# A hybrid decoder layer on one core: a fourth wide block product in the up projections, and a final norm split over two banks

## The chip, the cores and the metric

The kernel runs on one NeuronCore of a Trainium2 chip. The metric is the device time of one execution in microseconds (us). Five engines matter: TensorE (PE) multiplies matrices into PSUM banks, VectorE (DVE) and ScalarE (ACT) work on tiles of 128 rows, GpSimd (POOL) and SyncE (SP) issue transfers here. Each engine takes its instructions in the order in which the program gives them, and waits at one whose inputs aren't there yet.

## The reference, cut to what matters

One layer of 1024 columns over 512 positions in float32: a gated feed-forward block, a mixer, a second gated feed-forward block, and a root-mean-square norm. The change touches the up projections of both feed-forward blocks and the very end.

```python
def rmsnorm(x, g):
    x32 = x.astype(jnp.float32)
    y = x32 * lax.rsqrt(jnp.mean(x32 * x32, axis=-1, keepdims=True) + EPS)
    return (y * g.astype(jnp.float32)).astype(x.dtype)

def swiglu(x, w_gate, w_up, w_down):
    return (jax.nn.silu(x @ w_gate) * (x @ w_up)) @ w_down

x = x + 0.5 * swiglu(rmsnorm(x, ffn1_norm[l]), ffn1_wg[l], ffn1_wu[l], ffn1_wd[l])
x = x + hybrid_mixer(rmsnorm(x, mix_norm[l]), w_in[l], ...)
x = x + 0.5 * swiglu(rmsnorm(x, ffn2_norm[l]), ffn2_wg[l], ffn2_wu[l], ffn2_wd[l])
return rmsnorm(x, final_norm)
```

## The kernel before

*Three products for one.* Every float32 matrix is split into a rounded part and the rest: weights into `wh` (ACT copies, rounding) and `wl` (DVE subtracts: `wl = w - wh`), operands likewise into two halves of a tile `cm`: columns `lo` (0 to 255) hold the rounded part, columns `hi` (256 to 511) the rest. A product is `wh x lo + wh x hi + wl x lo`, three matmuls of 256 columns for a weight tile.

*Block products.* The up projection (`ffn_up`, L378) multiplies pairs of weight blocks by a scheme with seven block products instead of eight, numbered p = 1 to 7. A "set" `w` is one pair of blocks of the gate matrix (even `w`, `o.j` = 0) or of the up matrix (odd `w`, `o.j` = 1). The first projection has 16 sets, the second 18 (`count`). The list `stream` (L451 to 456) gives the order of the products of all sets: 1, 2 of set w, 4 of set w-1, 6 of w, 3 of w-1, 5 and 7 of w; each set adds seven. In the loop over `stream`, step i issues on PE the four weight tiles of product i (`products`, L482), then on ACT and DVE what follows from product i-1 (`results`, L510), then the split into `wh` and `wl` for product i+4 (`prepare`, L469; `LEAD` is 4), with the sum of weight blocks that the product after needs (`add_weights`, L459: `s`). In the first few rounds of 14 products one older result is split as well (`halve`, L600, every 14th step while i // 14 is under 6 in the first projection and under 4 in the second). The order is written out by hand, each engine's queue is the order of the program.

*Wide products.* Where `wide(p, w)` (L506) holds, the two matmuls that share `wh` are one of 512 columns over `lo` and `hi`, into both halves of a bank, and the halves are added later by DVE. Before, this is so for products 2, 5 and 3 (`WIDE`, L48), which have banks of the pool `aux`; product 4 goes, with 1, 6 and 7, into the bank `o.beta` of the pool `mm`, a running sum that ACT or DVE reads after each of them.

*What follows a product.* `o.t1` and `o.t2` hold a set's results (tiles `tg` for even sets, `tu` for odd ones). After product 4 an even set's Silu is taken by ACT from the bank, and an odd set's DVE multiplies the bank with the even set's Silu into `h2`. After product 3, ACT takes the Silu of `o.t1` (even) or DVE multiplies `h1` (odd).

*The end.* The second down projection ends with product 4 of its own block scheme, eight steps for row blocks m = 0 and 1; the last three (`TAIL`, L46) are done for m = 0 first and then for m = 1. Then (L1733 on) DVE adds each block's bank to the residual `xr`, the squares are summed (ACT for m = 0, DVE for m = 1), `norm_root` (L1682) takes the root on ACT and the reciprocal on DVE, and `scaled` (L1693) makes the two output halves of a row block, one on ACT and one on DVE, and issues their transfers.

Of the kernel before, what the change touches and what calls it, by code (L numbers as in the profile page):

```python
# [9 lines left out]
F32 = mybir.dt.float32  # L10
F32R = mybir.dt.float32r
AF = mybir.ActivationFunctionType
ALU = mybir.AluOpType

P = 128
S = 512
D = 1024
# [6 lines left out]
QB = 128  # L24
# [18 lines left out]
WARM = 8  # L43
HS = S // 2
LEAD = 4
PLAIN, PAIRS, TAIL = 6, 8, 3  # L46
DIRECT = 4
WIDE, FIRST_WIDE = (2, 5, 3), 2  # L48


ORDER = """
# [126 lines left out]
def hybrid_kernel(ctx, tc, xt, vec, w1u, w1d, wm, wki, wrg, watt, wrnn, wout, w2u, w2d, gf, out):  # L178
    nc = tc.nc
    plan = Plan()  # L180
    V, A = plan.engine("DVE", nc.vector), plan.engine("ACT", nc.scalar)
    G, T = plan.engine("POOL", nc.gpsimd), plan.engine("PE", nc.tensor)
    Q = plan.engine("SP", nc.sync)
# [16 lines left out]
    def nm(s):  # L200
        cnt[0] += 1
        return f"{s}_{cnt[0]}"

    def slot(dt=F32, name="s"):
        return plan.take("slot", big.tile([P, S], dt, tag="slot", name=nm(name)))

    def work(name="t", cols=S):
        return plan.take("tmp", tmp.tile([P, cols], F32, tag="tmp", name=nm(name)))

    def awork(name="a"):  # L210
        return patt.tile([P, S], F32, tag="att", name=nm(name))

    def psum(tag="mm"):
        return psp.tile([P, S], F32, tag=tag, name=nm(tag))
# [100 lines left out]
    lo, hi = slice(0, HS), slice(HS, S)  # L315
# [62 lines left out]
    def ffn_up(y, wu, n0, hs, g, waiting=(), given=(), ahead=None):  # L378
# [10 lines left out]
        ws = []  # L389
# [65 lines left out]
        w = count - 1  # L455
        stream[-3:] = [(5, w), (7, w), (3, w - 1), (4, w), (3, w)]
        units = []
# [52 lines left out]
        def results(i):  # L510
            p, w = stream[i]
            o = ws[w]
            if p == 1:
                o.t1, o.t2 = (work("tg"), work("tg")) if o.j == 0 else (awork("tu"), awork("tu"))
                A.activation(o.t1[:, lo], o.beta[:, lo], AF.Copy)
            elif p == 2:
                V.tensor_sub(o.t1[:, lo], o.p2[:, lo], o.t1[:, lo])
                if wide(2, w):
                    V.tensor_add(o.t1[:, lo], o.p2[:, hi], o.t1[:, lo])
            elif p == 6:  # L520
                A.activation(o.t1[:, hi], o.beta[:, lo], AF.Copy)
            elif p == 7:
                A.activation(o.t2[:, hi], o.beta[:, lo], AF.Copy)
                V.tensor_add(o.t2[:, hi], o.gamma[:, lo], o.t2[:, hi])
                if wide(5, w):
                    V.tensor_add(o.t2[:, hi], o.gamma[:, hi], o.t2[:, hi])
                if o.j:
                    o.h2 = slot(F32, "h")
                    V.tensor_mul(o.h2[:, hi], o.t2[:, hi], ws[w - 1].t2[:, hi])
                else:  # L530
                    A.activation(o.t2[:, hi], o.t2[:, hi], AF.Silu)
            elif p == 4:
                if o.j:
                    V.tensor_mul(o.h2[:, lo], o.beta[:, lo], ws[w - 1].t2[:, lo])
                else:
                    A.activation(o.t2[:, lo], o.beta[:, lo], AF.Silu)
            elif p == 3:
                V.scalar_tensor_tensor(o.t1[:, hi], o.gamma[:, lo], -1.0, o.t1[:, hi], op0=ALU.mult, op1=ALU.subtract)
                if wide(3, w):
                    V.tensor_sub(o.t1[:, hi], o.t1[:, hi], o.gamma[:, hi])  # L540
                if o.j:
                    o.h1 = slot(F32, "h")
                    V.tensor_mul(o.h1, o.t1, ws[w - 1].t1)
                    hs.extend((o.h1, o.h2))
                else:
                    A.activation(o.t1, o.t1, AF.Silu)

        with tc.manual_schedule(engines=ENGINES):
            for _ in range(len(raws), RAWS + len(raws)):
# [3 lines left out]
            for d, (n, j) in enumerate(direct):  # L553
# [5 lines left out]
                steps = [results_direct(d - 1)] if d else []  # L559
# [210 lines left out]
    for k in range(KD):  # L770
        if k:
            Q.dma_start(x[k], xt[k])
        if k % CH == 0:
            c = slice(k * P, (k + CH) * P)
# [14 lines left out]
    for k in range(KD):  # L789
        y.append(norm_tile(k, V_G1, False))  # L790
        if k % CH == 0:
            c = slice(k * P, (k + CH) * P)
# [4 lines left out]
    pu, w = psum(), given(AH[0])  # L797
# [86 lines left out]
    steps, index, last = d1.steps, d1.index, len(d1.steps) - TAIL  # L884
# [70 lines left out]
    with tc.manual_schedule(engines=ENGINES):  # L955
# [3 lines left out]
        for i in range(last):  # L959
            if i == 0:  # L960
                for k in ("pth", "ptl"):
                    t = ptp.tile([P, NQ * S], F32, tag=k, name=nm("sm"))
# [285 lines left out]
    for k in ("pth", "ptl"):  # L1248
        q = ptp.tile([P, NQ * S], F32R, tag=k, name=nm("QI"))
# [341 lines left out]
    steps, index, units, turned, tasks_at = d2.steps, d2.index, d2.units, d2.turned, d2.tasks_at  # L1591
# [15 lines left out]
    def chain(p, m):  # L1607

        key = CHAIN.get(p, p), m
        if key not in banks:  # L1610
            banks[key] = psum("aux" if p == 2 else "mm")
        return banks[key]

    def products(i, ms=range(2)):
        h, l = (t[:, i % 2 * S:(i % 2 + 1) * S] for t in units[i // 2])
        if steps[i][0] == "D":
            _, half, k = steps[i]
            hh, hl = hs[k]
            for m in range(NQ):
                if k == 0:  # L1620
                    banks["D", half, m] = psum("aux")
                c, o = slice(m * QB, (m + 1) * QB), banks["D", half, m]
                T.matmul(o, hh[:, c], h, start=k == 0, stop=False)
                T.matmul(o, hl[:, c], h, start=False, stop=False)
                T.matmul(o, hh[:, c], l, start=False, stop=k == PLAIN - 1)
            return
        p, j = steps[i]
        t, starts = turned[p, j], p in (1, 2, 5)
        opens = dict(skip_group_check=not starts)
        for m in ms:  # L1630
            o, th, tl = chain(p, m), t[:, m * QB:(m + 1) * QB], t[:, HS + m * QB:HS + (m + 1) * QB]
            T.matmul(o, th, h, start=starts and j == 0, stop=False, **opens)
            T.matmul(o, tl, h, start=False, stop=False, **opens)
            T.matmul(o, th, l, start=False, stop=j == PAIRS - 1, **opens)

    def rows(m, half):
        return xr[m // 2][:, m % 2, half * S:(half + 1) * S]

    def results(i):
        st = steps[i]  # L1640
        if st[0] == "D":
            if st[2] == PLAIN - 1:
                for m in range(NQ):
                    r = rows(m, st[1])
                    V.scalar_tensor_tensor(r, banks["D", st[1], m], 0.5, r, op0=ALU.mult, op1=ALU.add)
            return
        p, j = st
        if j == PAIRS - 1:
            for s_, half, sign in ADDS[p]:
                for m in range(2):  # L1650
                    r = rows(2 * s_ + m, half)
                    V.scalar_tensor_tensor(r, chain(p, m), 0.5 * sign, r, op0=ALU.mult, op1=ALU.add)

    gb = []
# [8 lines left out]
    def squares(m, half, ss, E=A):  # L1663
        sq, r = work("sq"), rows(m, half)
        if E is A:
            A.activation(sq, r, AF.Square, accum_out=ss)
        else:
            V.tensor_tensor_reduce(sq, r, r, 1.0, 0.0, ALU.mult, ALU.add, ss)

    norms = {}  # L1670
# [11 lines left out]
    def norm_root(m):  # L1682
        ss = norms[m]
        A.activation(ss[:, 3:4], ss[:, 2:3], AF.Sqrt, scale=1.0 / D, bias=ss[:, 1:2])
        rs = norms[m] = st_("rs", "m8")
        V.reciprocal(rs[:, 0:1], ss[:, 3:4])
# [6 lines left out]
    def scaled(m, E=Q):  # L1693

        rs, o = norms[m][:, 0:1], [slot(F32, "o") for _ in range(2)]
        A.activation(o[0], rows(m, 0), AF.Copy, scale=rs)
        E.dma_start(out[m * QB:(m + 1) * QB, :S], o[0])
        V.scalar_tensor_tensor(o[1], rows(m, 1), rs, gb[1], op0=ALU.mult, op1=ALU.mult)
        Q.dma_start(out[m * QB:(m + 1) * QB, S:], o[1])
# [14 lines left out]
    ffn_up(y2, w2u, 0, hs, V_G2, ahead=tasks_at)  # L1714
    with tc.manual_schedule(engines=ENGINES):
        assert min(d2.tasks) >= 0
        for i in range(len(steps) - TAIL):
            if i < KD // 2:
                turn(2 * i)
                turn(2 * i + 1)  # L1720
            products(i)
            if i:
                results(i - 1)
            if i == 8:
                gains()
            tasks_at(i)
            for f_, args in late.pop(i, ()):
                f_(*args)
        results(len(steps) - TAIL - 1)
        assert not late  # L1730

        for m in range(2):
            for i in range(len(steps) - TAIL, len(steps)):  # L1733
                products(i, (m,))
        for m in range(2):
            r = rows(m, 1)
            if m:
                norm_root(0)
            V.scalar_tensor_tensor(r, chain(4, m), 0.5, r, op0=ALU.mult, op1=ALU.add)
            squares(m, 1, norms[m][:, 2:3], (A, V)[m])  # L1740
        scaled(0, nc.scalar)
        norm_root(1)
        scaled(1, nc.scalar)


def _tiles(w, kt, m=P):
# [55 lines left out]
```

## Time and profile before

| | |
|---|---|
| time, median of 3 runs (lowest to highest) | 1063.77 us (1063.01 to 1063.98) |
| the profiled execution, its own time | 1063.79 us |
| its span in the profile | 1062.0 us |
| PE busy, of the span | 1052.5 us (99%) |
| DVE busy | 879.4 us (83%) |
| ACT busy | 665.3 us (63%) |
| granted TensorE clock, mean | 0.999 |

In rows of a timeline the first number is the start in us from the span's start, the second the time in us, then engine, line, operation, tiles written and read (`out<-in`), shape and count; in brackets the pause of the engine before it and what ended it. Nearly every row has line L172, that of the helper that records operations, so rows are told apart by their tiles: `wh`, `wl` are the parts of weights, `s` sums of weight blocks, `cm` operands, `mm` and `aux` PSUM banks, `tg` and `tu` results. A row with x2 joins two instructions. A row's time holds the operation's latency; back to back, the next one starts a little before the row ends. The view of stretches gives busy time of each engine with the count of instructions, then granted clock, share of the transfer engines, and GB/s.

### The profile page before, as it was taken

To read this page: it belongs to the slowest core of one execution; us is meant where nothing else is said; L and a number is where in the kernel's file an instruction comes from. 1 tells how busy PE (TensorE), PEld (TensorE's weight loads), DVE (VectorE), ACT (ScalarE), POOL (GpSimd) and SP (SyncE) were. 2 spreads that over 40 slices of the span, in tenths; PEclk is the share of its full clock that TensorE was granted. 3 is DMA by queue.
4 is the path that set the end of the run, shared out by engine and by line. 5 is a ranking of instruction groups with operands and counts; after the bars stand their busy time and mean duration, and the time that the engine had idled before them with its cause. 6 is when DMAs were issued, how large, how long until landed. Compare 5 with 4: busy or idle time off the path is not lost.

```text
span 1062.0 us, 17140 instructions
## 1 busy us (share of the span) xinstructions
PE 1052.5 (99%) x6068; PEld 926.2 (87%) x6068; DVE 879.4 (83%) x1734; ACT 665.3 (63%) x1311; POOL 171.5 (16%) x219
## 2 busy tenths in 40 slices
PE   9999999999999999999999999999999999999997
PEld 7889999999999888888888888888899999998885
DVE  6687898889978889899989867756878988878885
ACT  6575555555656668897896574446656555565753
POOL 0161111102430002110100000001611111101510
PEclk9999999999999999999999999999999999999999
DMA  7297677738993464343423211434977777548973
GB/s 279 60 258 184 175 197 175 186 107 235 259 206 97 132 172 124 105 124 106 138 80 99 81 31 54 143 112 110 247 188 172 189 197 165 154 120 257 256 160 120
DMA packets 73239, 165.98 MB, mean 156 GB/s; under 512 B 9024, under 2 KB 15296, under 8 KB 73152
## 3 DMA queue, kind: packets, MB, share of 16 engines
q1 hardware_dynamic: 46608, 119.72, 34.7%
q0 software_dynamic: 26112, 44.58, 24.2%
q8 instruction: 48, 0.79, 0.3%
q10 hardware_dynamic: 432, 0.57, 0.2%
q14 instruction: 39, 0.32, 0.1%
HBM read 151.73 MB, written 2.10 MB: 145 GB/s over the span
## 4 chain that ended last, share of the span: by engine, by line
PE 98%; DMA 0%; issue 0%; ACT 0%; DVE 0%; SPq 0%; ACTq 0%
PE mm L172 68%; PE aux L172 29%; DMA x<-xt 0%; ACT wh L172 0%; ACT yh L172 0%; SPq L160 0%; DVE o L172 0%; DVE yl L172 0%; DVE xr L172 0%; DVE acc L172 0%; DVE sq L172 0%; ACT sq L172 0%; DVE rs L172 0%; ACTq L172 0%; DVE ss L172 0%
## 5 line engine op out<-in xcount | busy, mean ns | idle before, releaser
L172 PE MATMUL mm<-cm,wh 128*128 128x256 f32 x1472 | 268.5, 283 | 0.0
L172 PEld LDWEIGHTS mm<-cm,wh 128*128 128x128 f32 x1472 | 229.1, 191 | 3.4 <-ACT tg L172 0.2
L172 DVE TENSOR_TENSOR wl<-wr,wh 128x512 fp32r<-128x512 f32 (+2 forms) x228 | 188.9, 832 | 45.9 <-ACT wh L172 44.2
L172 PE MATMUL mm<-cm,wl 128*128 128x256 f32 x736 | 208.4, 283 | 0.0
L172 ACT ACTIVATE wh<-wr 128x512 fp32r<-128x512 f32 (+3 forms) x230 | 167.9, 737 | 56.6 <-issue 21.5
L172 PE MATMUL mm<-yh,wh 128*128 128x512 f32 (+1 forms) x416 | 163.7, 394 | 0.7 <-ACT wh L172 0.7
L172 PE MATMUL mm<-yl,wh 128*128 128x512 f32 (+1 forms) x416 | 162.3, 390 | 0.0
L172 PE MATMUL aux<-cm,wh 128*128 128x512 f32 (+1 forms) x552 | 159.6, 351 | 0.0
L172 PE MATMUL mm<-yh,wl 128*128 128x512 f32 x408 | 159.2, 390 | 0.0
L172 PEld LDWEIGHTS mm<-cm,wl 128*128 128x128 f32 x736 | 140.4, 191 | 0.0
L172 ACT ACTIVATE wh<-s 128x512 fp32r<-128x512 f32 x152 | 92.9, 624 | 54.4 <-DVE s L172 42.1
L172 DVE TENSOR_TENSOR wl<-s,wh 128x512 fp32r<-128x512 f32 x152 | 103.5, 686 | 24.9 <-ACT wh L172 23.2
L172 PE MATMUL aux<-cm,wl 128*128 128x256 f32 x440 | 123.7, 281 | 0.0
L172 PEld LDWEIGHTS aux<-cm,wh 128*128 128x128 f32 x552 | 96.7, 189 | 12.8 <-DMA cm<-cb 0.2
L172 PEld LDWEIGHTS mm<-yh,wh 128*128 128x128 f32 (+1 forms) x416 | 77.9, 187 | 17.8 <-ACT wh L172 1.4
L172 PEld LDWEIGHTS mm<-yl,wh 128*128 128x128 f32 (+1 forms) x416 | 77.6, 187 | 16.0 <-DVE yl L172 0.8
L172 PEld LDWEIGHTS mm<-yh,wl 128*128 128x128 f32 x408 | 76.6, 188 | 16.5 <-DVE wl L172 0.2
L172 PEld LDWEIGHTS aux<-cm,wl 128*128 128x128 f32 x440 | 83.5, 190 | 0.0
L172 PE MATMUL mm<-wh,cm 128*128 128x512 f32 x192 | 59.1, 389 | 0.0
L172 ACT ACTIVATE tg<-tg 128x512 f32<-128x512 f32 (+1 forms) x44 | 24.1, 548 | 50.8 <-DVE tg L172 50.8
L160 POOL DMA_DIRECT2D s<-w2u x36 | 33.6, 1063 | 125.1 <-DVE wl L172 47.0
L160 POOL DMA_DIRECT2D cm<-cb x8 | 7.1, 888 | 266.3 <-DMA wr<-w2u 209.1
(243 smaller groups left out, 2063.7 us busy)
## 6 DMA issues: line engine op xcount, KB each, us to landing
wr<-wm SPq DMA_DIRECT2D x39, 512.0 KB, 3.6
wr<-w2u SPq DMA_DIRECT2D x26, 512.0 KB, 4.7
wr<-w1u SPq DMA_DIRECT2D x21, 512.0 KB, 5.4
wr<-w1d SPq DMA_DIRECT2D x18, 512.0 KB, 4.4
s<-w2u SPq DMA_DIRECT2D x36, 256.0 KB, 6.0
s<-w2u POOLq DMA_DIRECT2D x36, 256.0 KB, 5.1
wr<-w2d SPq DMA_DIRECT2D x18, 512.0 KB, 5.4
s<-w1u SPq DMA_DIRECT2D x32, 256.0 KB, 5.7
```

The costliest lines, as they stand in the source:

```text
L160: return self.engine.dma_start(out, src, **kw)
L172: return call(*args, **kw)
```

## The change

`WIDE` takes in product 4, for the sets in which 5 and 3 are wide already. After it ACT copies the bank's `lo` half and DVE adds the `hi` half to it; the Silu of an even set is taken by ACT after product 3, two products later, behind the Silu that stands there. At the end four steps instead of three are kept apart (`TAIL2`), block 1's products are done for its first 256 columns and then for its last 256, these into a new bank `rest` of the pool `aux`; the work of the last norm is written out in a new order, with outputs of block 0's halves on SP and block 1's second half in two pieces.

```diff
-PLAIN, PAIRS, TAIL = 6, 8, 3
+PLAIN, PAIRS, TAIL, TAIL2 = 6, 8, 3, 4
-WIDE, FIRST_WIDE = (2, 5, 3), 2
+WIDE, FIRST_WIDE = (2, 5, 3, 4), 2
...
+            elif p == 4 and wide(4, w):
+                A.activation(o.t2[:, lo], o.beta[:, lo], AF.Copy)
+                V.tensor_add(o.t2[:, lo], o.beta[:, hi], o.t2[:, lo])
+                if o.j:
+                    V.tensor_mul(o.h2[:, lo], o.t2[:, lo], ws[w - 1].t2[:, lo])
             elif p == 4:
                 if o.j:
                     V.tensor_mul(o.h2[:, lo], o.beta[:, lo], ws[w - 1].t2[:, lo])
...
                 else:
                     A.activation(o.t1, o.t1, AF.Silu)
+                    if wide(4, w):
+                        A.activation(o.t2[:, lo], o.t2[:, lo], AF.Silu)
...
-    def products(i, ms=range(2)):
-        h, l = (t[:, i % 2 * S:(i % 2 + 1) * S] for t in units[i // 2])
+    def products(i, ms=range(2), cols=slice(0, S), bank=None):
+        h, l = (t[:, i % 2 * S:(i % 2 + 1) * S][:, cols] for t in units[i // 2])
...
+        first = j == PAIRS - TAIL2 if bank is not None else starts and j == 0
         for m in ms:
-            o, th, tl = chain(p, m), t[:, m * QB:(m + 1) * QB], t[:, HS + m * QB:HS + (m + 1) * QB]
-            T.matmul(o, th, h, start=starts and j == 0, stop=False, **opens)
+            o, th, tl = (chain(p, m) if bank is None else bank)[:, cols], t[:, m * QB:(m + 1) * QB], t[:, HS + m * QB:HS + (m + 1) * QB]
+            T.matmul(o, th, h, start=first, stop=False, **opens)
...
-        for m in range(2):
-            for i in range(len(steps) - TAIL, len(steps)):
-                products(i, (m,))
-        for m in range(2):
-            r = rows(m, 1)
-            if m:
-                norm_root(0)
-            V.scalar_tensor_tensor(r, chain(4, m), 0.5, r, op0=ALU.mult, op1=ALU.add)
-            squares(m, 1, norms[m][:, 2:3], (A, V)[m])
-        scaled(0, nc.scalar)
+        tail = range(len(steps) - TAIL2, len(steps))
+        for i in tail:
+            products(i, (0,))
+        for i in tail:
+            products(i, (1,), lo)
+        rest = psum("aux")
+        for i in tail:
+            products(i, (1,), hi, rest)
+        r = rows(0, 1)
+        V.scalar_tensor_tensor(r, chain(4, 0), 0.5, r, op0=ALU.mult, op1=ALU.add)
+        squares(0, 1, norms[0][:, 2:3])
+        o1 = slot(F32, "o")
+        V.tensor_mul(o1, r, gb[1])
+        r, ss, sq = rows(1, 1), norms[1], work("sq")
+        V.scalar_tensor_tensor(r, chain(4, 1), 0.5, r, op0=ALU.mult, op1=ALU.add)
+        V.tensor_tensor_reduce(sq[:, lo], r[:, lo], r[:, lo], 1.0, 0.0, ALU.mult, ALU.add, ss[:, 2:3])
+        V.scalar_tensor_tensor(ss[:, 1:2], ss[:, 2:3], 1.0 / D, ss[:, 1:2], op0=ALU.mult, op1=ALU.add)
+        norm_root(0)
+        o0 = slot(F32, "o")
+        rs = norms[0][:, 0:1]
+        A.activation(o0, rows(0, 0), AF.Copy, scale=rs)
+        Q.dma_start(out[:QB, :S], o0)
+        V.scalar_tensor_tensor(r[:, hi], rest[:, hi], 0.5, r[:, hi], op0=ALU.mult, op1=ALU.add)
+        V.tensor_tensor_reduce(sq[:, hi], r[:, hi], r[:, hi], 1.0, 0.0, ALU.mult, ALU.add, ss[:, 2:3])
+        V.tensor_scalar(o1, o1, rs, None, op0=ALU.mult)
+        Q.dma_start(out[:QB, S:], o1)
         norm_root(1)
-        scaled(1, nc.scalar)
+        o0, o1, rs, c = slot(F32, "o"), slot(F32, "o"), norms[1][:, 0:1], out[QB:2 * QB]
+        A.activation(o0, rows(1, 0), AF.Copy, scale=rs)
+        nc.scalar.dma_start(c[:, :S], o0)
+        for q, h in enumerate((lo, hi)):
+            V.scalar_tensor_tensor(o1[:, h], r[:, h], rs, gb[1][:, h], op0=ALU.mult, op1=ALU.mult)
+            Q.dma_start(c[:, S + q * HS:S + (q + 1) * HS], o1[:, h])
```

More of the change, by code (lines that the diff above doesn't have):

```diff
@@ L1716, in hybrid_kernel @@
         assert min(d2.tasks) >= 0
-        for i in range(len(steps) - TAIL):
+        for i in range(len(steps) - TAIL2):
             if i < KD // 2:
@@ L1728, in hybrid_kernel @@
                 f_(*args)
-        results(len(steps) - TAIL - 1)
+        results(len(steps) - TAIL2 - 1)
         assert not late
-        for m in range(2):
-            for i in range(len(steps) - TAIL, len(steps)):
-                products(i, (m,))
-        for m in range(2):
-            r = rows(m, 1)
-            if m:
-                norm_root(0)
-            V.scalar_tensor_tensor(r, chain(4, m), 0.5, r, op0=ALU.mult, op1=ALU.add)
-            squares(m, 1, norms[m][:, 2:3], (A, V)[m])
-        scaled(0, nc.scalar)
-        norm_root(1)
-        scaled(1, nc.scalar)
+        tail = range(len(steps) - TAIL2, len(steps))
[24 more added lines that the diff above has]
+        Q.dma_start(out[:QB, S:], o1)
+        norm_root(1)
+        o0, o1, rs, c = slot(F32, "o"), slot(F32, "o"), norms[1][:, 0:1], out[QB:2 * QB]
[4 more added lines that the diff above has]
+            Q.dma_start(c[:, S + q * HS:S + (q + 1) * HS], o1[:, h])
 def _tiles(w, kt, m=P):
```

## The prediction

> **What bounds the kernel now.** I began with the page: the share of each engine and the chain that ended last.
>
> ```profile
> span 1062.0 us, 17140 instructions
> PE 1052.5 (99%) x6068; PEld 926.2 (87%) x6068; DVE 879.4 (83%) x1734; ACT 665.3 (63%) x1311; POOL 171.5 (16%) x219
> PE 98%; DMA 0%; issue 0%; ACT 0%; DVE 0%; SPq 0%; ACTq 0%
> ```
>
> TensorE (PE) sets the time almost everywhere. So a matmul saved in the up projections is worth its own time, unless VectorE (DVE), the next engine, falls behind. The second view is the busy time in two stretches of two weight sets each (14 block products, called a round below), one in the first up projection and a late one in the second.
>
> ```profile
> core 0: us, PE busy (x) PEld busy (x) DVE busy (x) ACT busy (x) POOL busy (x), PEclk, DMA share, GB/s
> 154.73:174.70 19.97, 19.97 (x146) 18.87 (x146) 17.88 (x36) 11.46 (x25) 3.52 (x4) 1.00 0.72 186
> 872.23:892.20 19.97, 19.97 (x146) 18.88 (x146) 17.28 (x33) 11.05 (x24) 3.52 (x4) 1.00 0.75 186
> ```
>
> A round takes 19.97 us and PE never rests. DVE is busy for 17.9 of it where an older result is also split (`halve`), 17.3 where none is. The 2.1 us left over look like room, so I read what ends each DVE pause in one round, from the timelines of DVE and of ScalarE (ACT).
>
> ```profile
> 157.66 1.38 DVE L172 TENSOR_TENSOR wl<-wr,wh 128x512 fp32r<-128x512 f32 x2
> 158.95 0.42 DVE L172 SCALAR_TENSOR_TENSOR tu<-aux,tu 128x256 f32<-128x256 f32 x1
> 159.40 0.42 DVE L172 TENSOR_TENSOR tu<-tu,aux 128x256 f32<-128x256 f32 x1
> ...
> 164.76 1.48 DVE L172 TENSOR_TENSOR wl<-s,wh 128x512 fp32r<-128x512 f32 x2 [1.01 <-ACT wh L172]
> ...
> 167.55 1.47 DVE L172 TENSOR_TENSOR wl<-wr,wh 128x512 fp32r<-128x512 f32 x2
> ...
> 169.39 0.42 DVE L172 TENSOR_TENSOR tg<-tg,aux 128x256 f32<-128x256 f32 x1
> 169.72 0.69 DVE L172 TENSOR_TENSOR s<-s,wr 128x512 f32<-128x512 f32 x1
> 171.03 0.69 DVE L172 TENSOR_TENSOR wl<-a,wh 128x512 fp32r<-128x512 f32 x1 [0.62 <-ACT wh L172]
> 171.64 0.69 DVE L172 TENSOR_TENSOR s<-s,wr 128x512 f32<-128x512 f32 x1
> ```
>
> ```profile
> 157.40 0.39 ACT L172 ACTIVATE tg<-mm 128x256 f32<-128x256 f32 x1 [1.80 <-PE mm L172]
> 157.68 0.62 ACT L172 ACTIVATE wh<-wr 128x512 fp32r<-128x512 f32 x1
> ...
> 163.78 0.42 ACT L172 ACTIVATE tg<-tg 128x256 f32<-128x256 f32 x1 [1.61 <-DVE tg L172]
> ...
> 169.84 0.63 ACT L172 ACTIVATE tg<-tg 128x512 f32<-128x512 f32 x1 [1.55 <-DVE tg L172]
> 170.38 0.61 ACT L172 ACTIVATE wh<-a 128x512 fp32r<-128x512 f32 x1
> ```
>
> This is the reading on which everything rests. DVE's two marked pauses, 1.01 and 0.62 us, are round trips: DVE writes `tg`, ACT takes its Silu, only then does ACT make the next `wh`, and DVE waits for that `wh`. If DVE runs later, ACT runs later with it, so these pauses are no room. Room is only where DVE waits for something that PE paces: ACT's copy at 157.40 waited for PE, then made `wh`, and the second of DVE's two `wl` waited for it. An undisturbed pair of such subtractions takes 1.29 us:
>
> ```profile
> 214.04 1.29 DVE L172 TENSOR_TENSOR wl<-s,wh 128x512 fp32r<-128x512 f32 x2
> ```
>
> So the pairs at 157.66 (1.38) and 167.55 (1.47) hide 0.09 and 0.18 us of waiting. DVE's own loop is 19.97 - 0.27 = 19.70 us: it is within 1.5% of being the bound, though its busy share says 83%.
>
> **How far DVE runs ahead.** The tightest place is the third block product (p 3) of an even set; its `wl` is the one written at 164.76, done 0.69 later at 165.45. PE's product starts:
>
> ```profile
> 162.90 0.40 PE L172 MATMUL aux<-cm,wh 128*128 128x512 f32 x1
> ...
> 164.31 0.40 PE L172 MATMUL mm<-cm,wh 128*128 128x256 f32 x2
> ...
> 167.19 0.40 PE L172 MATMUL aux<-cm,wh 128*128 128x512 f32 x1
> ```
>
> Product 3 starts at 167.19 and reads `wl` in its second matmul, some 0.23 later. DVE's lead is there 167.42 - 165.45 = 2.0 us.
>
> **The change, part by part.**
>
> *Wide products.* The rows above give a wide product (one 512-column and one 256-column matmul per weight tile, four tiles) as 164.31 - 162.90 = 1.41 us, and two plain ones (three 256-column matmuls per tile) as 167.19 - 164.31 = 2.88, 1.44 each. The fourth product becomes wide for sets 2 to count - 3: 12 of 16 in the first up projection, 14 of 18 in the second. Gain: 26 x 0.03 = 0.8 us, as long as PE is the bound; bounds 0.5 to 1.1, since rows have two digits. The Trainium skill, page "TensorE: Matmul & The Clock Gate", section "Back-to-back issue gap", puts a warm gap at columns / 2.4 plus 2.5 ns, by which joining two matmuls saves 2.5 ns and the 104 joined pairs would give an estimated 0.3 us instead; the trace, with 0.03 us per four, disagrees, and I go by the trace.
>
> *What DVE and ACT get for it.* A wide product leaves its result in two halves of a bank. Even set: before, ACT took the Silu straight from the bank (same place and form as `tg<-mm` above); now ACT copies (the same 0.28 us of queue), DVE adds the other half, and the Silu is a further ACT instruction two products on, right behind the 512-column Silu at 169.84. Odd set: ACT gains a copy, DVE an addition ahead of its multiplication. Each new addition is one of the 256-column kind: 0.34 us from start to start (169.39 to 169.72), 0.45 where the next one reads its result (158.95 to 159.40). Per round: 0.34 (even) + 0.45 (odd; the multiplication reads it) = 0.79 on DVE. The moved Silu stands between 169.84 and the `wh<-a` for which DVE pauses 0.62, and pushes that by 0.28 (157.40 to 157.68, start to start). The odd set's ACT copy is covered: ACT is busy 11.5 of 20 and waits there. DVE's loop becomes 19.70 + 0.79 + 0.28 = 20.77 us against PE's 19.97 - 0.06 = 19.91: a loss of 0.86 us per round where `halve` also splits a result, and 0.26 where not (0.60 less, the step from one subtraction to the next at 171.03 to 171.64). Queued behind each new addition are the `wl` of later products, for which PE waits once the lead is gone.
>
> *Adding up.* First projection: sets 2 to 13, tight product of sets 4, 6, 8, 10, 12, so five rounds, all with a split: 5 x 0.86 - 2.0 of lead = 2.3 us of PE stalls. Second projection: six rounds up to set 14; the split runs in the first three, 3 x 0.86 - 2.0 = 0.6, then 3 x 0.26 = 0.8: 1.4 us. What follows has spare DVE time, and a stall once taken isn't won back, as PE has no gap to close. Stalls: 3.7 us, between 1.5 (0.60 a round) and 6 (1.10 a round).
>
> *The end.* The path behind the last matmul:
>
> ```profile
> 1051.95 2.73 PE mm L172 x12
> 1054.71 0.70 DVE xr L172
> ...
> 1055.43 0.69 DVE sq L172
> 1056.13 0.01 DVE ss L172
> 1056.13 0.67 DVE o L172
> ...
> 1056.91 0.75 DVE o L172
> ```
>
> From DVE's start at 1054.71 to the end of the last output piece (1056.91 + 0.75 = 1057.66) are 2.95 us. In it stand 0.67 for an output of row block 0, ahead of the reciprocal for which block 1 waits. Now the last four products of block 1 are done by column halves, the second half in a bank of its own, so the first half's addition and squares run under the 1.44 us of the second half's 12 matmuls. Behind them remain, with the rows above halved: addition 0.4, squares 0.4, root, reciprocal and hand-overs 0.6 (estimated from the 0.78 between 1056.13 and 1056.91, of which block 0's 0.67 now lies partly under the root), then two half outputs of 0.4 to 0.5 each, of which the first leaves while the second is made. That is 2.3 to 2.5, a gain of 0.55. It costs 24 matmuls of 256 columns (1.44 / 12 = 0.12 each) for 12 of 512 (2.73 / 12 = 0.228): 0.15 us. The output leaves in five pieces instead of four, four of them issued on SP instead of two, block 0's first half among them, which moves there from ACT's queue. The trace shows no piece as small as 128 KB:
>
> ```profile
> DMA to landing us min/median/max: 2.0/2.1/3.2
> ```
>
> I bound it by these landings of 256 KB pieces: a gain of 0.4 if the last, halved, piece lands like half of what lies between 3.2 and 2.1, a loss of 0.3 if a fourth issue on SP queues; I take a gain of 0.1, nearer to none, as most landings are at the lower end already. End: -0.5 us, from -0.9 to 0.
>
> Sum: +3.7 - 0.8 - 0.5 = +2.4 us. The profiled execution took 1063.79 us (span 1062.0 and 1.8 around it) and the median is 1063.77, so I add to that: 1066.2 us.
>
> **The rivals.**
> *A, DVE keeps up.* If the 2.1 us that DVE isn't busy per round were real room, 0.79 would fit and the stalls vanish: -0.8 - 0.5 = 1062.5 us, not slower. For it: DVE's idle time is larger than what is added, and PE has never waited so far. Against it: both marked pauses are ended by ACT, behind work that DVE released. It decides as soon as the loss per round is under 2.0 / 5 = 0.4 us.
> *B, no lead to use up.* If the 2.0 us at product 3 are not all usable, because another product has less or because loads for later sets slip with DVE (POOL and SP wait for the buffers that DVE frees), every round's loss shows: 5 x 0.86 + 3 x 0.86 + 3 x 0.26 - 1.3 = +6.4, 1070.2 us. Against it: neighbouring products have `wl` done further ahead, and the loads are issued about a set early.
> *C, the end gives nothing.* The four issues on SP and the extra matmuls eat the shorter tail (0.2 us worse than now): with the stalls, 1063.8 + 3.7 - 0.8 + 0.2 = 1066.9 us. For it: more issues on one queue; against it: SP is otherwise empty there.
>
> **How the numbers follow.** Forecast as summed, 0.62, own range 1064.3 to 1068.3 (stalls 1.8 to 5.8, the rest as taken); A 0.20; C 0.10; B 0.08. The range 1062.3 to 1068.3 takes in A and leaves out B and the edges. What a measurement of this kernel can tell from no change is about 0.2%, 2.1 us: slower begins at 1065.9, which is inside the forecast's range, a little under its middle: 0.62 x 0.58 + 0.10 x 0.7 + 0.08 = 0.51 slower. Faster than 1061.6 would need more than A gives, 0.03. The rest, 0.46, is the same.
>
> **What would show it.** In the profile after, rounds of the early sets in the first projection at 19.91 us, the later ones at about 20.7; pauses of PE ahead of product 3 of even sets, ended by DVE `wl`; the DVE pause near `wl<-a` grown from 0.62 to 0.9 and the hidden 0.09 and 0.18 gone; in the second projection shorter stalls after the splits end. From the last matmul to the last issue 2.4 us instead of 2.95. I am wrong if PE still has no pause in either projection, if rounds stay at 19.9 to the end, or if stalls show from the first wide round on.

## The result, and the profile after

| | before | after |
|---|---|---|
| time, median of 6 runs (lowest to highest) | 1063.88 us (1062.55 to 1064.84) | 1068.49 us (1067.56 to 1069.55) |
| ratio to before, 95% interval | | 1.0045 (1.0032 to 1.0058) |
| span of the profiled execution | 1062.0 us | 1067.3 us |

The change makes the kernel 4.6 us slower. The forecast was slower by 2.4 us, 1066.2; the measured time is 2.3 us above that and just outside the range. First the page of the kernel after: the span, the share of each engine, and the chain that ended last.

```profile
span 1067.3 us, 17015 instructions
PE 1055.3 (99%) x5976; PEld 921.4 (86%) x5976; DVE 887.9 (83%) x1766; ACT 668.6 (63%) x1337; POOL 171.1 (16%) x219
PE 87%; DVE 7%; ACT 2%; issue 2%; DMA 2%; SPq 0%; DVEq 0%; POOLq 0%; ACTq 0%
```

PE still shows 99% and DVE 83%, as before. The chain tells more: PE held 98% of it and now holds 87%, and DVE, which had none, holds 7%.

I cut the trace into stages by PE's own rows: an up projection from its first matmul on block operands (`cm`) to the first matmul of the down projection, then to the last matmul, then to the end of the span. The second feed-forward block begins with plain products, from the first matmul on `yh` into `aux`.

| stage, us | before | after | difference |
|---|---|---|---|
| first up projection | 160.55 | 163.80 | +3.25 |
| from there to the second feed-forward block | 482.06 | 482.10 | 0.0 |
| its plain products, to the second up projection | 45.36 | 45.34 | 0.0 |
| second up projection | 181.13 | 183.51 | +2.38 |
| second down projection, to the start of the last matmul | 111.39 | 112.18 | +0.8 |
| from there to the end | 7.72 | 6.93 | -0.8 |

Both up projections lose, and the end gains what the last stage before it gives away. The rest of the difference between the spans (-0.3) is when the first inputs arrive: over all profiles here the first up projection starts between 73.1 and 74.5 us. So times are compared by medians, and places by stages.

The same view of stretches as before, of one round each: two in the first up projection, two in the second, where `halve` no longer runs in the last one.

```profile
core 0: us, PE busy (x) PEld busy (x) DVE busy (x) ACT busy (x) POOL busy (x), PEclk, DMA share, GB/s
146.14:166.93 20.79, 20.22 (x137) 18.45 (x137) 18.45 (x37) 11.86 (x27) 3.52 (x4) 1.00 0.68 180
166.93:187.72 20.79, 20.22 (x136) 18.44 (x136) 18.46 (x37) 11.85 (x27) 3.48 (x4) 1.00 0.69 178
841.90:862.69 20.79, 20.20 (x138) 18.43 (x137) 18.46 (x37) 11.83 (x26) 3.48 (x4) 1.00 0.72 180
882.80:902.97 20.17, 20.17 (x139) 18.42 (x138) 17.84 (x36) 11.30 (x25) 4.89 (x6) 1.00 0.72 185
```

A round takes 20.79 us instead of 19.97, and 20.17 without the split. The forecast had 20.77 and 20.17 as DVE's own loop, so from there on DVE's loop sets the pace. PE, which had no such pause before, has six now, four in the first projection and two in the second:

```profile
PE mm L172 <- ACT tu L172: 3.5, 6, 0.6
```

Now the place where PE pauses, from the timelines of the kernel after: of PE, of ACT and of DVE.

```profile
166.08 0.28 PE L172 MATMUL mm<-cm,wl 128*128 128x256 f32 x1
166.93 0.51 PE L172 MATMUL mm<-cm,wh 128*128 128x256 f32 x2 [0.57 <-ACT tu L172]
```

```profile
165.67 0.42 ACT L172 ACTIVATE tg<-tg 128x256 f32<-128x256 f32 x1 [1.61 <-DVE tg L172]
165.99 0.61 ACT L172 ACTIVATE wh<-s 128x512 fp32r<-128x512 f32 x1
166.51 0.36 ACT L172 ACTIVATE tu<-mm 128x256 f32<-128x256 f32 x1
...
171.87 0.94 ACT L172 ACTIVATE tg<-tg 128x512 f32<-128x512 f32 x2 [2.29 <-DVE tg L172]
```

```profile
166.64 1.48 DVE L172 TENSOR_TENSOR wl<-s,wh 128x512 fp32r<-128x512 f32 x2 [1.00 <-ACT wh L172]
...
169.43 0.42 DVE L172 TENSOR_TENSOR tg<-mm,tg 128x256 f32<-128x256 f32 x1
169.76 1.28 DVE L172 TENSOR_TENSOR wl<-wr,wh 128x512 fp32r<-128x512 f32 x2
...
173.36 0.69 DVE L172 TENSOR_TENSOR wl<-a,wh 128x512 fp32r<-128x512 f32 x1 [0.92 <-ACT wh L172]
```

A pause is worth more than the 0.57 us in the brackets, as the row ahead of it is drawn with its latency: from start to start the step is 0.85 us (166.08 to 166.93), where the same step takes 0.12 in the kernel before (165.63 to 165.75, below). The rounds without the split lose their 0.2 us at the same place, too little for the view to show it as a pause.

DVE's rows are as forecast. The new addition stands at 169.43. The pair at 169.76 takes 1.28 us, so its hidden 0.18 us of waiting is gone, and the second marked pause has grown from 0.62 to 0.92, since ACT's row at 171.87 now holds two Silus. But PE does not pause where I expected it. It waits ahead of product 6 of an odd set, and not for a `wl`: it waits for an ACT copy, `tu<-mm`. Products 1, 6, 7 and 4 of a set add up in the same 256 columns of one bank, and ACT copies the sum out after product 1. Product 6 must not write before that copy is done, and the copy stands in ACT's queue behind the Silu for which ACT waits on DVE. DVE late makes the Silu late, then the copy, then PE. In the kernel before, that copy and product 6 stand here:

```profile
164.63 0.37 ACT L172 ACTIVATE tu<-mm 128x256 f32<-128x256 f32 x1
...
165.63 0.28 PE L172 MATMUL mm<-cm,wl 128*128 128x256 f32 x1
165.75 0.40 PE L172 MATMUL mm<-cm,wh 128*128 128x256 f32 x2
```

The copy was done at 165.00 and PE came at 165.75: a lead of 0.75 us, not 2.0.

The end, from DVE's timeline of the kernel after:

```profile
1060.69 0.42 DVE L172 SCALAR_TENSOR_TENSOR xr<-aux,xr 128x256 f32<-128x256 f32 x1
1061.15 0.42 DVE L172 CUSTOM_DVE_ANT_0 sq<-xr 128x256 f32<-128x256 f32 x1
...
1061.50 0.48 DVE L172 TENSOR_SCALAR o<-o,rs 128x512 f32<-128x512 f32 x1
...
1062.14 0.88 DVE L172 SCALAR_TENSOR_TENSOR o<-xr,rs,gb 128x256 f32<-128x256 f32 x2
```

From DVE's start on the last bank (1060.69) to the end of the last output piece (1062.14 + 0.88) are 2.3 us, where there were 2.95.

### The profile page after: what moved, and what is told of

Read it like the earlier page. It is cut to its first block, busy times and chain, and to the rows that moved or that the text cites. A ratio compares the mean times of both kernels' runs of the same rounds, so it can differ in the third digit from the quotient of the medians.

```text
span 1067.3 us, 17015 instructions
## 1 busy us (share of the span) xinstructions
PE 1055.3 (99%) x5976; PEld 921.4 (86%) x5976; DVE 887.9 (83%) x1766; ACT 668.6 (63%) x1337; POOL 171.1 (16%) x219
## 4 chain that ended last, share of the span: by engine, by line
PE 87%; DVE 7%; ACT 2%; issue 2%; DMA 2%; SPq 0%; DVEq 0%; POOLq 0%; ACTq 0%
PE mm L172 62%; PE aux L172 25%; DVE wl L172 3%; DMA cm<-cb 1%; ACT wh L172 1%; DVE s L172 1%; DVE ca L172 1%; DVE tu L172 1%; DVE tg L172 1%; DVE h L172 0%; DMA x<-xt 0%; ACT cm L172 0%; DVE cb L172 0%; ACT tg L172 0%; DVE cm L172 0%
## 5 line engine op out<-in xcount | busy, mean ns | idle before, releaser
L172 PE MATMUL mm<-cm,wh 128*128 128x256 f32 (+1 forms) x1368 | 269.0, 293 | 3.5 <-ACT tu L172 3.5
L172 PEld LDWEIGHTS mm<-cm,wh 128*128 128x128 f32 x1368 | 216.3, 191 | 14.4 <-ACT tu L172 6.7
L172 DVE TENSOR_TENSOR wl<-wr,wh 128x512 fp32r<-128x512 f32 (+2 forms) x228 | 186.6, 831 | 40.6 <-ACT wh L172 40.0
L172 ACT ACTIVATE tg<-tg 128x256 f32<-128x256 f32 (+1 forms) x57 | 28.1, 515 | 59.5 <-DVE tg L172 59.5
L172 PE MATMUL mm<-wh,cm 128*128 128x512 f32 (+1 forms) x192 | 58.1, 385 | 0.0
```

What stands on the lines that cost most here:

```text
L172: return call(*args, **kw)
```

## The experiments

Three theories. *Loop*: DVE's own loop, with its round trips through ACT, is longer than PE's, and PE pays once a lead of 0.75 us at product 6 of odd sets is used up. *Bank*: the loss belongs to the bank that product 4 shares, however busy DVE is. *End*: the loss is in the last norm's new order. All runs below were timed; "before" is the kernel before beside them on the same chip.

**The wide product alone.** The change without its new end: `TAIL` and the old code behind it stay.

> The wide fourth product alone, with the old end. Theory Loop (DVE's own loop of 20.77 us per round of 14 products, with its round trips through ACT, is longer than PE's 19.91, and PE pays after a lead of about 0.75 us at product 6 of odd sets): all of the loss is here, 5.0 to 5.5 us over before (4.6 measured for the whole change, plus the 0.5 that the new end saves). Theory End (the loss is in the new order of the last norm): 0.8 us under before. Theory Bank (the loss comes from the bank that product 4 shares with 1, 6 and 7 being held longer): the same 5 us; other runs tell it apart.

Measured: 1069.27 us against 1063.44, ratio 1.0055 (1.0042 to 1.0067), 5.8 us over, a little more than expected. Up projections 163.83 and 183.49 us, as in the whole change. *End* falls.

**The end alone.**

```diff
-WIDE, FIRST_WIDE = (2, 5, 3, 4), 2
+WIDE, FIRST_WIDE = (2, 5, 3), 2
```

> The new end alone, product 4 plain. Loop and Bank: 0.5 us under before (1063.3), and the stretch from DVE's start on the last bank to the end of the last output piece is 1.9 to 2.4 us instead of 2.95. End: 4 us or more over before.

Measured: 1063.21 against 1063.44, ratio 0.9996 (0.9987 to 1.0004). A gain of 0.2 us that the interval doesn't tell from none. In the stages the last matmul starts 0.35 us later and the end is 0.70 shorter. The two parts do add up: 5.8 - 0.2 against 4.6, within what the intervals allow.

**PE's part alone.** Wide products and the new end, with the second half of product 4's bank left out of the result.

```diff
-            elif p == 4 and wide(4, w):
-                A.activation(o.t2[:, lo], o.beta[:, lo], AF.Copy)
-                V.tensor_add(o.t2[:, lo], o.beta[:, hi], o.t2[:, lo])
...
-                    if wide(4, w):
-                        A.activation(o.t2[:, lo], o.t2[:, lo], AF.Silu)
```

> The whole change, but the second half of the wide product 4's bank is left out of the result: ACT and DVE do after product 4 what they did before (Silu straight from the bank, or one multiplication). PE's work is that of the changed kernel. Loop: no loss, 0.8 + 0.5 = 1.3 us under before (1062.5), which is the price of the wide matmuls and of the end alone. Bank: still a loss, as the wide product writes the same bank, 2 us or more over before.

Measured: 1062.76 against 1063.44, ratio 0.9992 (0.9983 to 1.0001), and no pause of PE in the up projections. *Bank* falls as far as the matmuls go: the same ones write the same bank and nothing is lost. Against the end alone, it gains 0.45 us by the medians (11 runs each) and 0.18 + 0.21 by the two up projections: that is what the 26 wide products give, half of the 0.8 I had summed.

**Two additions more on the kernel before.** Nothing wide, only DVE work that no one reads.

```diff
             elif p == 4:
+                if FIRST_WIDE <= w < count - 2:
+                    V.tensor_add(acc[:, lo], rstd[:, lo], rstd[:, lo])
                 if o.j:
```

> The kernel before, with nothing wide added, and one extra DVE addition of 256 columns (on-chip tiles that nobody reads then) after each product 4 of sets 2 to count - 3, two per round. Loop: DVE's loop becomes 19.70 + 0.68 = 20.38 us against PE's 19.97, a loss of 0.41 a round where halve runs too and none where it doesn't; with a lead of 0.75 at product 6 that is 5 x 0.41 - 0.75 = 1.3 and 3 x 0.41 - 0.75 = 0.5, 1.8 us over before, with PE pausing ahead of product 6 of odd sets. Bank, and the reading of DVE's busy share as room (17.9 + 0.7 of 20): no pause, the time of before.

Measured: 1064.99 against 1063.53, ratio 1.0013 (1.0004 to 1.0022), 1.5 us over; the first up projection is 1.1 us longer, the second 0.1 (1.3 and 0.5 expected). PE pauses at the named place, in a kernel without the change:

```profile
186.31 0.51 PE L172 MATMUL mm<-cm,wh 128*128 128x256 f32 x2 [0.16 <-ACT tu L172]
```

**Four additions more.** As above, and a second one on the other halves of the same tiles.

> As the run with two extra additions per round on the kernel before, now four. Loop: 19.70 + 1.36 = 21.06 us a round, a loss of 1.09 with halve and 0.49 without: 5 x 1.09 - 0.75 = 4.7 and 3 x 1.09 - 0.75 + 3 x 0.49 = 4.0 us, 8.7 over before, six times what two additions cost (1.4), since a lead is used up once. If each extra addition just cost its share: twice 1.4, 2.9 us over before. DVE's busy share as room (17.9 + 1.4 of 20): nothing more than noise.

Measured: 1071.55 against 1063.84, ratio 1.0071 (1.0059 to 1.0084), 7.7 us over, five times the cost of two. The view of stretches gives one of its rounds, between two of PE's pauses:

```profile
146.95:167.98 21.03, 20.24 (x145) 18.92 (x145) 19.04 (x39) 11.15 (x25) 3.51 (x4) 1.00 0.74 182
```

The round is 21.03 us (21.06 expected), with DVE busy for 19.04 of it. The cost is not a price per instruction: it is what exceeds PE's round, less a lead that is spent once per projection.

**ACT's copy first.** The copy after product 1 of an odd set goes ahead of the Silu that waits for DVE.

```diff
+        def first_copy(o):
+            if not hasattr(o, "t1"):
+                o.t1, o.t2 = (work("tg"), work("tg")) if o.j == 0 else (awork("tu"), awork("tu"))
+                A.activation(o.t1[:, lo], o.beta[:, lo], AF.Copy)
...
                 else:
+                    if i + 1 < len(stream) and stream[i + 1][0] == 1:
+                        first_copy(ws[w + 1])
                     A.activation(o.t2[:, hi], o.t2[:, hi], AF.Silu)
```

> The whole change, with ACT's copy of product 1 of odd sets put ahead of the Silu for which ACT waits on DVE, instead of behind it; the same instructions, one moved. Loop with the lead of 0.75 us at product 6 of odd sets: that wait goes, the next lead is that of product 3, 2.0 us, and DVE's loop loses the 0.2 us for which a wh stood behind that copy: 5 x 0.66 - 2.0 = 1.3 us of pauses in the first projection and about none in the second, so 0.4 us over before (0 to 1.2). If the lead didn't matter and DVE's loop alone set the time from the first wide round on: 4 us over before, nearly unchanged.

Measured: 1066.43 against 1063.53, ratio 1.0025 (1.0015 to 1.0036): 2.9 us over, above the expected range. The up projections do nearly what was expected, +1.6 and -0.25 us instead of +3.25 and +2.4, so the lead at that copy is what the changed kernel lacked. But the second down projection is 2.0 us longer than before, with a pause in its first step:

```profile
947.74 0.50 PE L172 MATMUL aux<-wh,hh 128*128 128x512 f32 x1 [1.42 <-DVE tu L172]
```

PE waits there for DVE to finish reading an up result of the same pool of banks. Two things make DVE late. One is a lag that PE no longer paid on the way: DVE begins the step ahead of the last Silu (`tg<-aux`) 0.96 us before the down projection starts (943.03 and 943.99), in the changed kernel 2.0 us before it (946.18 and 948.19). The other is that ACT's queue differs here in more than the moved copy: copies for the next stage (`xr<-mm`) stand ahead of the last Silu, while in the changed kernel they stand behind it and two `wh`.

```profile
943.08 0.66 ACT L172 ACTIVATE xr<-mm 128x256 f32<-128x256 f32 x2 [1.55 <-PE aux L172]
944.27 0.39 ACT L172 ACTIVATE xr<-mm 128x256 f32<-128x256 f32 x1 [0.54 <-PE mm L172]
944.55 0.62 ACT L172 ACTIVATE tg<-tg 128x512 f32<-128x512 f32 x1
945.07 1.14 ACT L172 ACTIVATE wh<-wr 128x512 fp32r<-128x512 f32 x2
```

DVE waits 2.28 us for that `wh` (1.22 in the changed kernel). So by estimate 1.1 us of the loss at this place are the order and 0.5 the lag, as PE's step is 1.82 us long instead of 0.24; how the order came about is not known. A longer lead defers part of a lag to the next stage; only spare time of DVE removes it.

**The moved Silu behind the next `wh`.** The order of ACT's queue is changed for that one instruction: in each step it is issued behind `prepare(i + LEAD)` instead of in `results`.

```diff
                     if wide(4, w):
-                        A.activation(o.t2[:, lo], o.t2[:, lo], AF.Silu)
+                        behind.append((o.t2[:, lo], o.t2[:, lo]))
...
                     halve(hs, f0 + i + LEAD - len(stream))
+                for t, src in behind:
+                    A.activation(t, src, AF.Silu)
+                behind.clear()
```

> The whole change, only the moved Silu of 256 columns put behind the next wh on ACT; the other two Silus stay. Loop: the 0.28 us by which it lengthened DVE's second pause goes, the loop is 20.49 against 19.94, 5 x 0.55 - 0.75 = 2.0 and 3 x 0.55 - 0.75 = 0.9 us of pauses, 1.9 us over before (1.3 to 2.6). Bank or a count of DVE's instructions: unchanged, 4.6 over before.

Measured: 1065.10 against 1063.53, ratio 1.0015 (1.0006 to 1.0023), 1.6 us over. 0.28 us of an instruction on an engine that is 63% busy were worth 3 us.

**The Silu taken at once.** In the branch of the wide product 4, an even set's Silu right behind the addition; none after product 3.

```diff
                 if o.j:
                     V.tensor_mul(o.h2[:, lo], o.t2[:, lo], ws[w - 1].t2[:, lo])
+                else:
+                    A.activation(o.t2[:, lo], o.t2[:, lo], AF.Silu)
```

> The whole change with the Silu of even sets taken at once, right behind DVE's addition, instead of two products later. Loop: a third round trip DVE, ACT, DVE of about 1.0 us a round comes in and the 0.28 goes: loop 21.5 us, 5 x 1.53 - 0.75 = 6.9 and 3 x 1.53 - 0.75 + 3 x 0.93 = 6.6 us of pauses, some 12 us over before (9 to 15). A count of DVE's and ACT's instructions: the same numbers as in the changed kernel, so 4.6 over before.

Measured: 1079.36 against 1063.53, ratio 1.0148 (1.0135 to 1.0162), 15.8 us over, 0.8 above the expected range; the instructions are those of the changed kernel. DVE has a third marked pause, and PE waits double as long in each round:

```profile
173.88 1.48 DVE L172 TENSOR_TENSOR wl<-wr,wh 128x512 fp32r<-128x512 f32 x2 [1.01 <-ACT wh L172]
```

```profile
169.96 0.51 PE L172 MATMUL mm<-cm,wh 128*128 128x256 f32 x2 [1.14 <-ACT tu L172]
```

**All Silus behind the next `wh`.** The same `behind` list for the three Silus after products 7 and 3.

```diff
-                    A.activation(o.t2[:, hi], o.t2[:, hi], AF.Silu)
+                    behind.append((o.t2[:, hi], o.t2[:, hi]))
...
-                    A.activation(o.t1, o.t1, AF.Silu)
+                    behind.append((o.t1, o.t1))
```

> The whole change, with every Silu after products 7 and 3 (the moved one too) put on ACT behind the next wh instead of ahead of it. Loop: both marked pauses of DVE (1.0 and 0.9 us a round) go, the loop falls to about 18.9 us, under PE's 19.91, PE has no pause and the time is 1.3 us under before (1062.5); rounds take 19.91 us from the first to the last. Bank: nothing about the bank changes, so 4 to 5 us over before. If only the count of DVE's instructions mattered (its busy share, not its round trips): unchanged against the changed kernel, 1068.5.

Measured: 1062.64 against 1063.44, ratio 0.9992 (0.9983 to 1.0001): 0.8 us under, where 1.3 had been expected. All 5 to 6 us of loss are gone, with DVE doing as much per round as in the changed kernel, and reading the shared bank as it does there, so *Bank* falls for the reading too:

```profile
150.77:170.71 19.94, 19.94 (x138) 18.44 (x138) 18.44 (x37) 12.45 (x27) 2.69 (x4) 1.00 0.75 185
```

**Once more, with two neighbours.** First the same kernel again, as the interval above left open whether it beats the kernel before.

> The same kernel as the whole change with all Silus behind the next wh, timed again beside its two neighbours: 0.9 us under before (0.4 of it from the wide products, 0.3 to 0.5 from the end).

Measured: 1062.23 against 1063.84, ratio 0.9984 (0.9975 to 0.9993): faster than the kernel before, by 0.8 and 1.6 us in the two comparisons; only the second is clear of no change.

The kernel before with its two Silus behind the next `wh`, nothing wide:

> The kernel before, with its Silus after products 7 and 3 behind the next wh and nothing else changed. Loop: DVE's pauses go, but PE has no pause to lose, so the time of before within 0.3 us. If the pauses of DVE cost time already in the kernel before: 0.5 us or more under it.

Measured: 1063.68 against 1063.84, ratio 0.9996 (0.9987 to 1.0005). DVE's round trips cost nothing in the kernel before, as PE had nothing to gain; they matter only once DVE is the longer loop.

All Silus behind, and wide products from the first set on (`FIRST_WIDE = 0`):

> The whole change with all Silus behind the next wh, and in addition wide products from the first set on instead of the third (products 2, 3, 4, 5 of sets 0 and 1, 16 more wide products in the two projections). If PE is the bound there too: 16 x 0.02 = 0.3 us under the same kernel without this (1062.3 against 1062.6). If DVE, busy with the operands at the start of a projection, is late there: 0.5 to 2 us over it.

Measured: 1062.40 against 1063.84, ratio 0.9989 (0.9980 to 0.9997), beside 1062.23 without it. The up projections are shorter by 0.16 and 0.27 us in the profile, the times don't show it: left undecided.

## Why the prediction was wrong

*That DVE is close to the bound, and why.* Right, and the reason held in every run: pauses that are round trips through ACT are no room. Rival A, which took DVE's idle time for room, is refuted by the kernel before with additions: 1.4 us of DVE work a round in 2.1 us of idle time cost 7.7 us.

*The loop after the change.* Right: 20.77 and 20.17 us forecast, 20.79 and 20.17 measured; the 0.28 of the moved Silu is seen in the pause (0.62 to 0.92) and, alone, in the run that moves it.

*How far DVE runs ahead.* This is the step that failed. I looked for the lead only where PE waits for DVE's own output, and took 2.0 us at product 3. The tighter one runs through ACT: the copy of a running sum, behind the Silu, with 0.75 us at product 6 of odd sets. Put into the same sum, 5 x 0.86 - 0.75 = 3.5 us and 3 x 0.86 - 0.75 + 3 x 0.26 = 2.6 us; the stages give 3.25 and 2.38 longer projections, 3.45 and 2.6 with the gain of the wide products put back. So 6.1 us of pauses instead of 3.7. That this copy was the place is shown by the run that moves it ahead: 1.7 and 2.6 us come off the two up projections. A second point of the same step was missing: what DVE lags behind at the end of a projection is not always free. In that run some 0.5 us of it is paid in the second down projection (the estimate above), where the prediction counted on spare DVE time.

*The wide products' gain.* Mis-sized: 0.8 forecast, about 0.4 measured (the round of 19.94 against 19.97, and the run without the addition). That is below my own lower bound of 0.5, and the two digits of the rows were not the reason: product 4 takes 1.44 us plain (164.31 to 165.75) and 1.42 wide (164.86 to 166.28 in the run with all Silus behind), not the 1.41 of the products that were wide already, and product 5 takes 1.42 (169.13 to 170.55) where it took 1.41 (168.59 to 170.00). Why is not shown. The Trainium skill's figure in "TensorE: Matmul & The Clock Gate", section "Back-to-back issue gap", from which I had worked out 0.3 us and set it aside, was nearer.

*The end.* 0.5 us forecast. The path behind the last bank is 2.3 us, as forecast (2.3 to 2.5), but alone the new end gave only 0.2 us in time, within the noise, and 0.35 in the stages: within its bounds. The stages bear its terms out. The last matmul is 0.11 us shorter by its row (0.28 for 0.39), so of the 0.70 us by which the time from its start to the end fell, 0.59 are the new end's (0.55 forecast), and of the 0.35 us by which it starts later, 0.24 are a cost (0.15 forecast). For the landings (0.1) no run shows a gain: from the last output piece to the end of the span it is 4.36 us before, 4.27 after and 4.40 with the end alone. The prediction says that the trace shows no piece as small as 128 KB; that holds for outputs alone, as weights do come in such pieces (`wr<-w1u`, 3.9 us to landing). Rival C, no gain at the end, is not refuted by the times.

*Rival B, no lead at all*, would have been 1070.2; the truth lies between it and the forecast, as the lead is between 0 and 2.0.

Corrected sum: 6.1 - 0.4 - 0.4 = +5.3 us, against 4.6 in the medians and 5.3 in the spans. That the spans agree so well is luck: the up projections alone are 5.6 us longer, the second down projection and the end give nothing together (+0.8 and -0.8), and the first up projection starts 0.35 us earlier in that profile. What hides the end's gain is 0.4 us more in the second down projection than the new end explains, where PE's weight loads wait for an ACT `wh` and a DVE `wl` (0.4 us each). The same two waits, and 0.66 us more in that stage, are in the profile of the kernel before with only its Silus moved, so they need no wide product; where they come from was not tried and stays open.

## What to carry to other kernels

Read an engine's room from what ends its pauses, not from its busy share: a pause ended by an engine that was itself waiting for this one moves along with it. Look for the shortest lead over every wait of the bound engine, those for a free buffer included, since a running sum that another engine copies out between products ties the two together. In an in-order queue, put what waits for another engine behind what that other engine is waiting for: moving three Silus behind the next `wh` gave back more than the whole loss.

## What the runs showed of the hardware that was not expected

Joining two matmuls of 256 columns into one of 512 with the same weights saves little: 0.39 us for 104 pairs by the two up projections without and with the 26 wide products (0.45 by the medians), about 4 ns each.
